# Softmax division, LayerNorm steps, row maximum and load buffers in the attention stage of a streaming encoder layer

## The chip, the cores and the metric

The kernel runs on one core of one Trainium2 chip. A core has a matrix engine (TensorE, PE in the profile; its weight loads are PEld), a vector engine (VectorE, DVE), an activation engine (ScalarE, ACT), a general engine (GpSimd, POOL) and a queue processor (SyncE, SP) which here issues all transfers. The metric is the time of one execution in microseconds (us), lower is better.

## The reference

One layer of a hybrid encoder runs over 1024 prompt frames and 64 sample frames (with 128 cached frames before them), 1088 columns in all. Shown is what matters here:

```
h = x + 1/2 * SwiGLU_1(RMSNorm(x))
u = RMSNorm(h); z = u @ W_in        # q, k, v, indexer q/k/weights, conv input, branch gates
attn:  every query keeps its top-k keys by indexer score, then
       p = softmax(q k^T / 8 over the kept keys); o = p v      # 8 heads of 64, 2 key/value heads
conv:  c = GLU(conv_in); dc = depthwise causal conv(c, width 31)
       conv_out = silu(LayerNorm(dc)) @ conv_w_out             # LayerNorm over 512 channels
merged = sigmoid(g_a) * (attn @ attn_w_out) + sigmoid(g_c) * conv_out
h = h + merged @ W_out
h = h + 1/2 * SwiGLU_2(RMSNorm(h))
y = RMSNorm(h)
```

All is float32. The kernel gets float32 accuracy out of the matrix engine by splitting each operand into a high part and a low remainder (ScalarE copies the high part, VectorE or GpSimd subtracts it) and adding three products: high x high, high x low, low x high (lines 136, 137, 138).

## The kernel before

Channels lie on the 128 partitions, frames along the free axis. Frames are worked in three chunks of 364, 362 and 362 columns (CHUNKS). Weights come tile by tile from DRAM (`raw`), and are split into `whi` (ScalarE, line 118) and `wlo` (GpSimd, line 119).

The program has these stages: the first feed-forward block, the input projection with convolution and indexer, the search for the top-k threshold, then the attention stage, and the second feed-forward block. The change lies in the attention stage alone.

**Attention.** There are nine query tiles (ATILES, in the order TORD = 7, 6, 8, 5, 4, 3, 2, 1, 0; tile i < 8 has 128 queries and 128(i + 1) keys, tile 8 has 64 queries and 192 keys) and four pairs of heads in each: 36 units, class Pair. A unit goes through three functions:

- `soft` (line 1189): for each of the two heads, and for one or two blocks of keys (two blocks when there are more than 512 keys), PE writes logits into a PSUM tile `lg` (lines 1209, 1210; there are three such tiles), and one VectorE instruction (line 1212) adds the mask `bias`, writes `pr` and gives the row maximum of the block into `mb`. Then the maximum is scaled into `mx` (lines 1218, 1220), ScalarE takes the exponential with a row sum `sm` (line 1222), VectorE inverts `sm` (line 1224), and the two heads are divided: the first by GpSimd (line 1225), the second by ScalarE (line 1226).
- `turn` (line 1229): PE transposes up to two blocks of keys of both heads into `pt` (line 1236; two PSUM tiles), and `pt` is split into `ph` (ScalarE) and `pl` (VectorE), both under lines 152 and 153. One such portion is a slot.
- `values` (line 1248): PE multiplies with the values (lines 1256, 1257) into `pv` (one PSUM tile); ScalarE and VectorE make `oh` (lines 1262, 1263), and SP stores it into `d_at` (line 1264).

`attention` (line 1268) runs `soft` two units ahead of `turn` (AHEAD = 2) and `values` two slots behind it (LAG = 2). After each slot it calls `fill`, which runs background steps from a list of five parts, in order. RATE says how many steps go with a slot in each part: 0.5, 1, 1, 0.5, 1.

**The background parts.** 1: `gate_part`, the last four gate projections (three chunks each, 12 steps, lines 1156 to 1164) and the LayerNorm of chunk 2. 2: `conv_part`, `conv_out` of chunks 2, 1, 0 (eight steps each) with the LayerNorms of chunks 1 and 0. 3: `merge` of chunk 2. 4: `wout` of chunk 2. 5: `merge` of chunk 1. What is left runs after the attention. A generator's `yield` ends a step.

`norm` (line 1292) works on the four channel tiles of one chunk: it loads `lx` (line 1298) and adds pairs of tiles on GpSimd (line 1299); takes column sums on PE (lines 166 and 1302) and the mean `mu`; subtracts it and squares, four tiles (lines 1308, 1309), and adds (line 1310); takes column sums again and an inverse square root (lines 185 to 191); and then for four tiles scales, applies swish by tanh and splits into `ch` and `cl` (lines 1321 to 1330), which `conv_out` multiplies with its weights. `both` joins two generators, one step of the second to each step of the first:

```
def both(a, b):
    for _ in a:
        next(b, None)
        yield
    for _ in b:
        yield
```

`conv_out` loads a gate row into `gc`, multiplies, stores it in `d_mp`. `merge` loads `ga` and `mpt`, adds both branches, and splits the sum into `xh` and `xl`. `wout` loads a row `hr` of h, adds to it, and stores it. `gc`, `ga`, `mpt` and `hr` have two buffers each.

**The order of the work** is not that of the program text. A planner reorders instructions on each engine by a priority (program order, and blocks marked as more urgent, such as the weight loads) and by a simulated time line with estimated durations, in which an instruction can be taken once its inputs and its buffers are free. The order it finds is fixed in the program; on the chip each engine works through its own queue in that order and waits where an input is late. All transfers go through the one queue of SP.

Of the kernel before, what the change touches and what calls it, by code (L numbers as in the profile page):

```python
# [9 lines left out]
F32 = mybir.dt.float32  # L10
# [82 lines left out]
class Kern:  # L93
# [432 lines left out]
    def run(self):  # L526
        tc, nc, a = self.tc, self.nc, self.a
        PS = bass.MemoryType.PSUM
        with ExitStack() as top:
# [659 lines left out]
            def soft(u):  # L1189

                rows, L = u.rows, u.L
                if u.h0 == 0 and u.i not in qts:
                    qts[u.i] = load_q(ak, d_q, u.t0, rows)
                qt = qts[u.i]
                nb = 2 if L > 512 else 1
                pw = L // nb
                mb = ap_.tile([P, 2, 2], F32, name="mb", tag="mb", bufs=AHEAD + 1)
                mx = ap_.tile([P, 2], F32, name="mx", tag="mx", bufs=AHEAD + 1)
                sm = ap_.tile([P, 2], F32, name="sm", tag="sm", bufs=AHEAD + 1)
                u.pr = []  # L1200
                kh, kl = K[u.g]
                for hh in range(2):
                    p = ap_.tile([P, 1024], F32, name="pr", tag="pr", bufs=2 * AHEAD + 2)[:rows, :L]
                    u.pr.append(p)
                    q = qt[:, u.h0 + hh, :rows]
                    for b in range(nb):
                        o = lgp.tile([P, 512], F32, name="lg", tag="lg")[:rows, :pw]
                        ks = u.k0 + b * pw
                        nc.tensor.matmul(o, q, kh[:, ks:ks + pw], start=True, stop=False)
                        nc.tensor.matmul(o, q, kl[:, ks:ks + pw], start=False, stop=True)  # L1210
                        bo = BOFF[u.i] + b * pw
                        nc.vector.tensor_tensor_reduce(p[:, b * pw:(b + 1) * pw], o, bias[:rows, bo:bo + pw],
                                                       1.0, -3e38, op0=ALU.add, op1=ALU.max,
                                                       accum_out=mb[:rows, hh, b:b + 1])
                        if (hh, b) == (1, nb - 1):
                            mm = mb[:rows, :, 0]
                            if nb == 2:
                                nc.vector.tensor_tensor(mx[:rows, :], mm, mb[:rows, :, 1], op=ALU.max)
                                mm = mx[:rows, :]
                            nc.vector.tensor_scalar(mx[:rows, :], mm, -0.125, None, op0=ALU.mult)  # L1220
                            for e in range(2):
                                nc.scalar.activation(u.pr[e], u.pr[e], AF.Exp, bias=mx[:rows, e:e + 1],
                                                     scale=0.125, accum_out=sm[:rows, e:e + 1])
                            nc.vector.reciprocal(sm[:rows, :], sm[:rows, :])
                            nc.gpsimd.tensor_scalar(u.pr[0], u.pr[0], sm[:rows, 0:1], None, op0=ALU.mult)
                            nc.scalar.activation(u.pr[1], u.pr[1], AF.Copy, scale=sm[:rows, 1:2])
                        yield

# [63 lines left out]
            def norm(c, lp_, cp_):  # L1292

                c0, w = CHUNKS[c]
                wd = w if c < 2 else w + 30
                x = lp_.tile([P, 4, 392], F32, name="lx", tag="lx")[:, :, :wd]
                s = lp_.tile([P, 4, 392], F32, name="ls", tag="ls")[:, :, :wd]
                nc.sync.dma_start(x, d_dc[:, :, c0:c0 + wd].rearrange("t p w -> p t w"))
                nc.gpsimd.tensor_tensor(s[:, 0:2, :], x[:, 0:2, :], x[:, 2:4, :], op=ALU.add)
                yield  # L1300
                mu = lp_.tile([P, 4], F32, name="mu", tag="mu", bufs=2)
                v = self.colsum([s[:, t, :] for t in range(2)], wd)[:, :, 0]
                mu = mu[:, :v.shape[1]]
                nc.vector.tensor_scalar(mu, v, -1.0 / 512, None, op0=ALU.mult)
                yield
                m = self.spread(mu, wd)
                for t in range(4):
                    nc.vector.tensor_tensor(x[:, t, :], x[:, t, :], m, op=ALU.add)
                    nc.scalar.activation(s[:, t, :], x[:, t, :], AF.Square)
                nc.gpsimd.tensor_tensor(s[:, 0:2, :], s[:, 0:2, :], s[:, 2:4, :], op=ALU.add)  # L1310
                yield
                yield
                y = self.rsqrt(self.colsum([s[:, t, :] for t in range(2)], wd), 1.0 / 512, lp_)
                yield
                yield
                r = self.spread(y, wd)
                ch = cp_.tile([P, 4, WMAX], F32R, name="ch", tag="ch")
                cl = cp_.tile([P, 4, WMAX], F32R, name="cl", tag="cl")
                C[c] = ch, cl
                for t in range(4):  # L1320
                    nc.vector.scalar_tensor_tensor(x[:, t, :], x[:, t, :], par("lng", t), r,
                                                   op0=ALU.mult, op1=ALU.mult)
                    nc.scalar.activation(s[:, t, :], x[:, t, :], AF.Tanh, bias=hb[:, 16 + t:17 + t], scale=0.5)
                    nc.scalar.activation(x[:, t, :], x[:, t, :], AF.Identity, bias=par("lnb", t))
                    nc.vector.scalar_tensor_tensor(x[:, t, :], s[:, t, :], 1.0, x[:, t, :],
                                                   op0=ALU.add, op1=ALU.mult)
                    parts = [(0, w, 0)] if c < 2 else [(0, SEQ - c0, 0), (SEQ - c0, w, 30)]
                    for a0, a1, sh in parts:
                        self.split(ch[:, t, a0:a1], cl[:, t, a0:a1], x[:, t, a0 + sh:a1 + sh],
                                   nc.vector if t % 2 else nc.gpsimd)  # L1330
                yield

            def conv_out(c, lp_):
                c0, w = CHUNKS[c]
                ch, cl = C[c]
                for m in range(8):
                    if m % 2 == 0:
                        wt = self.wload(wc[m // 2], 1024)
                    p = self.psum()[:, :w]
                    self.proj(p, wt, lambda k: ch[:, k, :w], lambda k: cl[:, k, :w], 4, (m % 2) * 512)  # L1340
                    gc = lp_.tile([P, WMAX], F32, name="gc", tag="gc", bufs=2)[:, :w]
                    nc.sync.dma_start(gc, d_g[8 + m, :, c0:c0 + w])
                    nc.vector.scalar_tensor_tensor(gc, gc, 1.0, p, op0=ALU.add, op1=ALU.mult)
                    nc.sync.dma_start(d_mp[m, :, c0:c0 + w], gc)
                    yield
# [7 lines left out]
            def merge(c, mp_):  # L1353
# [9 lines left out]
                for m in range(8):  # L1363
                    if m % 2 == 0:
                        wt = self.wload(wa[m // 2], 1024)
                    ga = mp_.tile([P, WMAX], F32, name="ga", tag="ga", bufs=2)[:, :w]
                    nc.sync.dma_start(ga, d_g[m, :, c0:c0 + w])
                    mpt = mp_.tile([P, WMAX], F32, name="mpt", tag="mpt", bufs=2)[:, :w]
                    nc.sync.dma_start(mpt, d_mp[m, :, c0:c0 + w])
                    p = self.psum()[:, :w]  # L1370
                    self.proj(p, wt, lambda k: ah[:, k, :], lambda k: al[:, k, :], 4, (m % 2) * 512)
                    nc.vector.scalar_tensor_tensor(p, ga, 1.0, p, op0=ALU.add, op1=ALU.mult)
                    nc.vector.scalar_tensor_tensor(ga, mpt, 0.5, p, op0=ALU.mult, op1=ALU.add)
                    self.split(mh[:, m, :w], ml[:, m, :w], ga)
                    yield
# [12 lines left out]

            def h_dram(pool):
                def row(m, c0, w):  # L1390
                    x = pool.tile([P, WMAX], F32, name="hr", tag="hr", bufs=2)[:, :w]
                    nc.sync.dma_start(x, d_h[:, m, c0:c0 + w])
                    return x, lambda: nc.sync.dma_start(d_h[:, m, c0:c0 + w], x)
                return row
# [6 lines left out]
            def both(a, b):  # L1401
                for _ in a:
                    next(b, None)
                    yield
                for _ in b:
                    yield
# [2 lines left out]

            def gate_part():  # L1410
                steps = gates(gorder[GPRE:], ak, 2)
                for _ in range(3 * (16 - GPRE) - 7):
                    next(steps)
                    yield
                lp = C["pool"] = self.pool(cx, "ln", 1)
                yield from both(norm(2, lp, lp), steps)
                act_es.close()

            def conv_part():
# [236 lines left out]
```

## Time and profile before

| | |
|---|---|
| median of 3 runs | 2339.89 us (2335.2 to 2342.22) |
| the profiled execution | 2337.39 us, of which its span is 2335.6 us |
| busy in the span | PE 2250.3, DVE 1689.2, ACT 1390.8, POOL 1499.4 us |
| mean granted clock of TensorE | 0.988 |
| attention stage | about 1180 to 1510 us of the span |

The span goes from the first to the last instruction of the program. A row of a stretch gives its bounds and length, then busy time and count for PE, PEld, DVE, ACT and POOL, the granted clock, the share of the transfer engines and GB/s. A row of a time line gives start, duration, engine, line, operation, output and inputs; in brackets stands the idle time of the engine just before, and what ended it. A row of a group gives the busy time and the mean duration in ns behind the first bar, and the idle time before these instructions with what ended it behind the second. A row for one line gives minimum, median and maximum in ns. A row of waits says who waited for whom, with total us, number of times and the longest.

### The profile page before, as it was taken

The numbers are of one execution on the slowest core, as the hardware profiler recorded it, in microseconds if no ns is written. First come the engines' busy times: TensorE is split into PE (matmuls) and PEld (weight loads), VectorE is DVE, ScalarE is ACT, GpSimd is POOL, SyncE is SP. The second block draws the span as 40 slices with busy tenths as digits, with TensorE's granted clock in tenths as the row PEclk, the third lists the DMA queues.
The fourth block names the chain that finished last, engine by engine and source line by source line (L and its number), as shares of the span: only waits on it lengthen the run. The fifth ranks groups of instructions, "written<-read, shape, count | busy, mean of one in ns | idle before, by whom it ended". The sixth has DMA issues, their size and how long they took to land. (4 is left out here: it accounts for less than half of the span.)

```text
span 2335.6 us, 44194 instructions
## 1 busy us (share of the span) xinstructions
PE 2250.3 (96%) x16226; PEld 2213.6 (95%) x16226; DVE 1689.2 (72%) x3868; ACT 1390.8 (60%) x2883; POOL 1499.4 (64%) x1039
## 2 busy tenths in 40 slices
PE   7999999999999999999999999899999999999997
PEld 6999999999999999999988889899999999999997
DVE  7887766787776388689956777467877757887765
ACT  6655555666546454897446767447656556556553
POOL 5677755677757593788723555467667756667664
PEclk9999999999999999999999999999999999999998
DMA  5322233223223443334322455753223232323233
GB/s 189 109 100 100 100 100 108 99 95 109 100 93 132 143 133 120 93 110 138 120 67 74 144 171 176 238 199 114 91 91 109 95 115 72 112 103 105 100 100 111
DMA packets 129548, 273.40 MB, mean 117 GB/s; under 512 B 17840, under 2 KB 77104, under 8 KB 129328
## 3 DMA queue, kind: packets, MB, share of 16 engines
q1 hardware_dynamic: 129328, 270.56, 35.1%
q8 instruction: 127, 2.08, 0.4%
q14 instruction: 93, 0.76, 0.1%
HBM read 231.82 MB, written 38.75 MB: 116 GB/s over the span
## 5 line engine op out<-in xcount | busy, mean ns | idle before, releaser
L136 PE MATMUL ps<-x,wp 128*128 128x272 f32 x1760 | 508.5, 290 | 7.1 <-ACT spare L342 3.3
L138 PE MATMUL ps<-x,wp 128*128 128x272 f32 x1760 | 504.1, 291 | 3.0 <-DVE wp L153 1.9
L137 PE MATMUL ps<-x,wp 128*128 128x272 f32 x1760 | 506.4, 288 | 0.0
L136 PE MATMUL ps<-x,whi 128*128 128x272 f32 (+2 forms) x1544 | 481.9, 312 | 6.0 <-ACT x L152 2.2
L153 POOL TENSOR_TENSOR wp<-s,wp 128x512 fp32r<-128x512 f32 x272 | 364.9, 1354 | 190.1 <-ACT wp L152 188.2
L138 PE MATMUL ps<-x,wlo 128*128 128x272 f32 (+2 forms) x1544 | 480.7, 312 | 0.0
L137 PE MATMUL ps<-x,whi 128*128 128x272 f32 (+2 forms) x1334 | 411.7, 309 | 1.0 <-POOL x L153 1.0
L327 POOL TENSOR_TENSOR wlo<-raw,whi 128x1024 fp32r<-128x1024 f32 x120 | 290.0, 2417 | 186.2 <-ACT whi L326 172.7
L119 POOL TENSOR_TENSOR wlo<-raw,whi 128x1024 fp32r<-128x1024 f32 (+1 forms) x123 | 279.1, 2272 | 176.8 <-ACT whi L118 166.3
L136 PEld LDWEIGHTS ps<-x,wp 128*128 128x128 f32 x1760 | 331.4, 189 | 11.9 <-ACT spare L342 5.7
L138 PEld LDWEIGHTS ps<-x,wp 128*128 128x128 f32 x1760 | 328.5, 188 | 6.1 <-DVE wp L153 4.0
L137 PEld LDWEIGHTS ps<-x,wp 128*128 128x128 f32 x1760 | 331.9, 189 | 0.0
L136 PEld LDWEIGHTS ps<-x,whi 128*128 128x128 f32 x1544 | 292.2, 189 | 9.1 <-ACT x L152 2.6
L138 PEld LDWEIGHTS ps<-x,wlo 128*128 128x128 f32 x1544 | 292.3, 189 | 1.2
L137 PEld LDWEIGHTS ps<-x,whi 128*128 128x128 f32 x1334 | 253.1, 190 | 2.4 <-POOL x L153 1.3
L152 ACT ACTIVATE wp<-s 128x512 fp32r<-128x512 f32 x272 | 168.0, 626 | 136.3 <-DVE s L314 75.5
L784 POOL TENSOR_TENSOR ac<-ac,pd 128x559 f32<-128x559 f32 (+1 forms) x132 | 192.5, 1459 | 22.8 <-ACT pd L783 15.4
L152 ACT ACTIVATE wp<-ps 128x512 fp32r<-128x512 f32 x208 | 123.2, 592 | 113.6 <-DVE ps L312 100.5
L439 DVE SCALAR_TENSOR_TENSOR h<-ps,h 128x272 f32<-128x272 f32 x448 | 174.1, 429 | 12.9 <-PE ps L138 12.4
L137 PE MATMUL ps<-gl,whi 128*128 128x272 f32 x640 | 183.4, 292 | 0.0
L137 PE MATMUL ps<-gl,wp 128*128 128x272 f32 x640 | 180.9, 288 | 0.0
L136 PE MATMUL ps<-gh,wp 128*128 128x272 f32 x640 | 178.8, 290 | 1.9 <-DVE h L439 1.8
(289 smaller groups left out, 5831.4 us busy)
## 6 DMA issues: line engine op xcount, KB each, us to landing
raw<-wf SPq DMA_DIRECT2D x353, 512.0 KB, 3.3
d_g<-sg SPq DMA_DIRECT2D x32, 181.0 KB, 1.9
d_h<-h SPq DMA_DIRECT2D x2, 2176.0 KB, 10.0
y<-t SPq DMA_DIRECT2D x32, 136.0 KB, 1.8
raw<-wf SPq DMA_DIRECT2D x16, 256.0 KB, 2.6
raw<-d_q SPq DMA_DIRECT2D x32, 128.0 KB, 3.7
raw<-d_qi SPq DMA_DIRECT2D x24, 128.0 KB, 3.0
d_g<-sg SPq DMA_DIRECT2D x16, 182.0 KB, 2.7
```

The lines of the kernel that those rows point to most:

```text
L119: self.weng.tensor_tensor(lo[:, :n], raw[:, :n], hi[:, :n], op=ALU.subtract)
L136: t.matmul(out, wh, xh, start=first, stop=False, skip_group_check=onto)
L137: t.matmul(out, wh, xl, start=False, stop=False, skip_group_check=onto)
L138: t.matmul(out, wl, xh, start=False, stop=last, skip_group_check=onto)
L152: nc.scalar.activation(hi, x, AF.Copy)
L153: (eng or nc.vector).tensor_tensor(lo, x, hi, op=ALU.subtract)
L327: self.weng.tensor_tensor(lo, raw, hi, op=ALU.subtract)
L439: nc.vector.scalar_tensor_tensor(x, p, 0.5, x, op0=ALU.mult, op1=ALU.add)
L784: nc.gpsimd.tensor_tensor(ac, ac, pd, op=ALU.add)
```

## The change

Four edits, all in the attention stage:

- In `soft`, the second block of a head takes the first block's maximum (in `mb`) as the starting value of its own maximum, so the last block's `mb` is the maximum of the row. The two VectorE instructions of lines 1218 and 1220 go; one ScalarE instruction scales `mb` into `mx`. The first head is divided by ScalarE instead of GpSimd.
- In `norm`, a step ends after two of the four tiles of the subtraction and after each of the first three tiles of the last part: it has 11 yields instead of 7.
- `both` takes two steps of the second generator for each step of the first (it now serves `conv_out` with `norm`). In `gate_part`, one gate step goes alone instead of five, and then each step of `norm` comes with one gate step; that makes 12 steps as before.
- `gc`, `ga`, `mpt` and `hr` have three buffers each.

```diff
@@ soft
                         nc.vector.tensor_tensor_reduce(p[:, b * pw:(b + 1) * pw], o, bias[:rows, bo:bo + pw],
-                                                       1.0, -3e38, op0=ALU.add, op1=ALU.max,
+                                                       1.0, mb[:rows, hh, 0:1] if b else -3e38,
+                                                       op0=ALU.add, op1=ALU.max,
                                                        accum_out=mb[:rows, hh, b:b + 1])
                         if (hh, b) == (1, nb - 1):
-                            mm = mb[:rows, :, 0]
-                            if nb == 2:
-                                nc.vector.tensor_tensor(mx[:rows, :], mm, mb[:rows, :, 1], op=ALU.max)
-                                mm = mx[:rows, :]
-                            nc.vector.tensor_scalar(mx[:rows, :], mm, -0.125, None, op0=ALU.mult)
+                            nc.scalar.activation(mx[:rows, :], mb[:rows, :, nb - 1], AF.Copy, scale=-0.125)
                             for e in range(2):
                                 nc.scalar.activation(u.pr[e], u.pr[e], AF.Exp, bias=mx[:rows, e:e + 1],
                                                      scale=0.125, accum_out=sm[:rows, e:e + 1])
                             nc.vector.reciprocal(sm[:rows, :], sm[:rows, :])
-                            nc.gpsimd.tensor_scalar(u.pr[0], u.pr[0], sm[:rows, 0:1], None, op0=ALU.mult)
+                            nc.scalar.activation(u.pr[0], u.pr[0], AF.Copy, scale=sm[:rows, 0:1])
                             nc.scalar.activation(u.pr[1], u.pr[1], AF.Copy, scale=sm[:rows, 1:2])
@@ norm
                     nc.scalar.activation(s[:, t, :], x[:, t, :], AF.Square)
+                    if t == 1:
+                        yield
                 nc.gpsimd.tensor_tensor(s[:, 0:2, :], s[:, 0:2, :], s[:, 2:4, :], op=ALU.add)
...
                         self.split(ch[:, t, a0:a1], cl[:, t, a0:a1], x[:, t, a0 + sh:a1 + sh],
                                    nc.vector if t % 2 else nc.gpsimd)
+                    if t < 3:
+                        yield
                 yield
@@ conv_out; the same in merge for ga and mpt, in h_dram for hr
-                    gc = lp_.tile([P, WMAX], F32, name="gc", tag="gc", bufs=2)[:, :w]
+                    gc = lp_.tile([P, WMAX], F32, name="gc", tag="gc", bufs=3)[:, :w]
@@ both
                 for _ in a:
                     next(b, None)
+                    next(b, None)
                     yield
@@ gate_part
-                for _ in range(3 * (16 - GPRE) - 7):
+                for _ in range(3 * (16 - GPRE) - 11):
                     next(steps)
                     yield
                 lp = C["pool"] = self.pool(cx, "ln", 1)
-                yield from both(norm(2, lp, lp), steps)
+                ns = norm(2, lp, lp)
+                for _ in ns:
+                    next(steps, None)
+                    yield
                 act_es.close()
```

More of the change, by code (lines that the diff above doesn't have):

```diff
@@ L1365, in merge @@
                         wt = self.wload(wa[m // 2], 1024)
-                    ga = mp_.tile([P, WMAX], F32, name="ga", tag="ga", bufs=2)[:, :w]
+                    ga = mp_.tile([P, WMAX], F32, name="ga", tag="ga", bufs=3)[:, :w]
                     nc.sync.dma_start(ga, d_g[m, :, c0:c0 + w])
-                    mpt = mp_.tile([P, WMAX], F32, name="mpt", tag="mpt", bufs=2)[:, :w]
+                    mpt = mp_.tile([P, WMAX], F32, name="mpt", tag="mpt", bufs=3)[:, :w]
                     nc.sync.dma_start(mpt, d_mp[m, :, c0:c0 + w])
@@ L1390, in row @@
                 def row(m, c0, w):
-                    x = pool.tile([P, WMAX], F32, name="hr", tag="hr", bufs=2)[:, :w]
+                    x = pool.tile([P, WMAX], F32, name="hr", tag="hr", bufs=3)[:, :w]
                     nc.sync.dma_start(x, d_h[:, m, c0:c0 + w])
```

## The prediction

> **What bounds the kernel now.** I read the page first, then stretches by stage.
>
> ```profile
> span 2335.6 us, 44194 instructions
> PE 2250.3 (96%) x16226; PEld 2213.6 (95%) x16226; DVE 1689.2 (72%) x3868; ACT 1390.8 (60%) x2883; POOL 1499.4 (64%) x1039
> ```
> ```profile
> core 0: us, PE busy (x) PEld busy (x) DVE busy (x) ACT busy (x) POOL busy (x), PEclk, DMA share, GB/s
> 1180.00:1260.00 80.00, 76.14 (x485) 73.75 (x484) 43.66 (x124) 46.68 (x77) 28.07 (x12) 0.96 0.18 58
> 1260.00:1400.00 140.00, 125.29 (x806) 115.84 (x804) 103.85 (x292) 97.15 (x202) 71.93 (x40) 0.95 0.49 146
> 1400.00:1510.00 110.00, 97.20 (x606) 93.46 (x607) 69.60 (x183) 69.31 (x154) 57.19 (x34) 0.96 0.64 197
> 1600.00:2336.00 736.00, 716.35 (x5633) 710.69 (x5631) 541.12 (x1184) 422.10 (x919) 478.94 (x331) 0.99 0.30 101
> ```
> PE sets the pace: outside the attention stage it is idle a few per cent at a clock of 0.99. The change touches 1180 to 1510, where PE is idle 3.9 + 14.7 + 12.8 = 31.4 us and the clock is down to 0.95. No edit removes PE work, so the gain can only come from idle PE and lost clock. Next, the single waits of PE, in order of time, and three stretches at half clock:
>
> ```profile
> start us, us, engine line op out<-in xcount [idle before <-releaser]
> 1276.38 0.59 PE L136 MATMUL ps<-ch,whi 128*128 128x362 f32 x2 [2.42 <-ACT ch L152]
> 1280.90 0.48 PE L1236 MATMUL pt<-ident,pr 128*128 128x128 f32 x1 [3.02 <-DVE pl L153]
> ...
> 1319.18 0.45 PE L1209 MATMUL lg<-kh,qt 128*128 128x384 f32 x1 [1.15 <-DVE mb L1212]
> 1323.65 0.69 PE L1236 MATMUL pt<-ident,pr 128*128 128x128 f32 x2 [2.07 <-POOL pr L1225]
> ...
> 1338.35 0.82 PE L166 MATMUL ps<-ones,ls 128*128 128x128 f32 x5 [1.02 <-POOL ls L1299]
> ...
> 1370.73 0.77 PE L136 MATMUL ps<-ch,whi 128*128 128x364 f32 x2 [1.82 <-ACT ch L152]
> ...
> 1422.49 0.44 PE L1209 MATMUL lg<-kh,qt 128*128 128x384 f32 x1 [1.45 <-DVE mb L1212]
> 1433.28 0.38 PE L1209 MATMUL lg<-kh,qt 128*128 128x256 f32 x1 [1.87 <-DVE mb L1212]
> ```
> ```profile
> 1278.80:1285.70 6.90, 4.80 (x19) 4.73 (x19) 4.57 (x9) 3.34 (x9) 3.63 (x6) 0.51 0.61 188
> 1323.20:1326.60 3.40, 2.95 (x12) 2.95 (x13) 0.83 (x4) 3.38 (x10) 3.40 (x3) 0.50 0.02 5
> 1371.00:1374.40 3.40, 2.92 (x13) 2.48 (x13) 3.34 (x7) 3.40 (x8) 3.23 (x3) 0.50 0.24 61
> ```
> The waits of 1276, 1319 to 1323 and 1370 are the ends of the three LayerNorms, where all four tiles are normalised in one background step; each is followed by half clock. At half clock half of PE's busy time is lost: (4.80 + 2.95 + 2.92) / 2 = 5.3 us.
>
> **The change part by part.** *LayerNorm in single tiles.* The same instructions are issued; between tiles now lies other work. At 1276 conv_out waits 2.42 for the last `ch`; with one tile per step only that tile's chain is left, I take 1.8 back. At 1280 the transposes wait 3.02 behind `cl` on DVE:
>
> ```profile
> L153 DVE TENSOR_TENSOR cl<-lx,ch x8: 316/720/2524, 1277.0 to 1375.2; 128x298 fp32r<-128x298 f32 x2, 128x64 fp32r<-128x64 f32 x2, 128x362 fp32r<-128x362 f32 x2, 128x364 fp32r<-128x364 f32 x2
> ```
> The slowest took 2.52 against a median of 0.72; with the four no longer in one heap I take 2.1 back. At 1319 I take half of 1.15 (0.6). At 1338 and 1370 the next norm runs two steps per conv_out step and is done two steps ahead of its reader: 1.0 and 1.8. Together 7.3 us. What is moved in the queues: each of the two later norms sends its one load to SP earlier among the loads and stores of conv_out, and its POOL additions and subtractions earlier among the weight subtractions, about 2 us each; conv_out's own transfers wait that much longer, covered by its two to three buffers, at no cost as long as the weights are loaded some steps ahead. If that cover were gone, the next weight would be late by one POOL subtraction, some 2 us. The first norm starts four gate steps sooner; its load and first addition stand at 1150 already (rival 3), so that alone changes nothing.
>
> *Both divides on ScalarE.*
>
> ```profile
> L1225 POOL TENSOR_SCALAR pr<-pr,sm 128x1024 f32<-128x1024 f32 (+8 forms) x36 | 60.8, 1691 | 99.7 <-DVE sm L1224 80.5 <-PE pt L1236 6.7 <-DVE ps L191 2.5
> L1226 ACT ACTIVATE pr<-pr,sm 128x1024 f32<-128x1024 f32 (+8 forms) x36 | 26.4, 735 | 6.1 <-DVE sm L1224 6.0
> L552 ACT ACTIVATE hb<-par x2: 189/194/198, 15.6 to 15.7; 128x16 f32<-128x16 f32 x1, 128x4 f32<-128x4 f32 x1
> 1360.00:1380.00 20.00, 17.33 (x104) 15.25 (x103) 17.78 (x43) 18.62 (x39) 11.15 (x7) 0.91 0.41 122
> ```
> POOL loses 60.8 us, off the path but for the 2.07 at 1323, where ACT would itself need about one more divide: I take 2.07 - 0.74 = 1.3, rounded down to 1.1. ACT gains 36 divides of 0.735 (26.4) and 36 `mx` scalings at the 0.19 of the small `hb` rows (7.0): 33.4 us in 330, or 2.0 in every 20. ACT's free time covers it (43 us in 1260 to 1400, 41 in 1400 to 1510), but 18.62 of 20 at 1360 leaves nothing over. Queued behind a divide on ACT stand the evictions of transposes (`ph`), on which PE's next values wait. Bounds: 0 to half exposed (17); I take 2, nearer the cover.
>
> *Running row maximum.*
>
> ```profile
> L1220 DVE TENSOR_SCALAR mx<-mb 128x2 f32<-128x2 f32 (+1 forms) x20 | 9.8, 492 | 0.1
> L1218 DVE TENSOR_TENSOR mx<-mb 128x2 f32<-128x2 f32 x16 | 5.8, 364 | 0.2
> L1220 DVE TENSOR_SCALAR mx<-mx 128x2 f32<-128x2 f32 x16 | 4.0, 248 | 0.2
> 1430.29 2.16 DVE L1220 TENSOR_SCALAR mx<-mb 128x2 f32<-128x2 f32 x1
> 1430.06 2.37 POOL L119 TENSOR_TENSOR wlo<-raw,whi 128x1024 fp32r<-128x1024 f32 x1
> 1353.85 0.16 DVE L190 SCALAR_TENSOR_TENSOR rt<-rt,ps 128x3 f32<-128x3 f32 x1
> 1354.04 0.17 DVE L191 SCALAR_TENSOR_TENSOR ps<-rt,ps 128x3 f32<-128x3 f32 x1
> 1357.85 0.07 DVE L1212 DVE_READ_ACCUMULATOR2_ANT mb<- 128x1 f32 x1
> 1357.85 0.48 DVE L1212 CUSTOM_DVE_ANT_0 pr<-lg,bias 128x320 f32<-128x320 f32 x1
> ```
> DVE loses 9.8 + 5.8 + 4.0 = 19.6 us. Two numbers a row cost up to 2.16, and that one ended with the 2.37 of POOL's weight subtraction: it held `mb`, and so the 1.87 of PE at 1433. In exchange the second reduction of a head (32 of them: four tiles, four pairs, two heads) must wait for the accumulator of the first. Independent ones start with the read of 0.08; dependent small ones (1353.85, 1354.04) stand 0.03 apart after the end: 32 x 0.11 = 3.5 us. The net 16 us of DVE lies beside PE: nothing but the wait at 1433.
>
> The Trainium skill (SBUF — State Buffer, Who interferes with whom) says that a GpSimd instruction and a DVE instruction that reads SBUF through both ports shut each other out for a whole instruction, while ACT never waits; the 2.16 agrees. By that rule alone the divide's going would also free all of DVE from POOL; the weight subtractions (2.37) stay, so the sum does not take it.
>
> *Three buffers.* At 1422 DVE sat behind a load of `ga`, and `lg` behind DVE:
>
> ```profile
> DVE ps L1372 <- DMA ga<-d_g: 4.9, 6, 1.7
> DVE hr L1385 <- DMA hr<-d_h: 13.5, 3, 4.9
> SPq L1369 <- DVE ga L1373: 6.8, 7, 2.0
> SPq L1367 <- DVE oh L1263: 7.2, 3, 3.2
> 1440.00:1480.00 40.00, 39.82 (x255) 39.42 (x253) 14.43 (x37) 19.59 (x35) 25.57 (x14) 1.00 0.61 188
> ```
> A third buffer frees the 6.8 that SP waits for a slot, not the 7.2 behind an attention store. `hr` waits 13.5, but in 1440 to 1480 PE is never short (39.82 of 40): nothing. Of 1.45 + 1.87 = 3.3 at 1422 and 1433 I take 2.5.
>
> *Sum.* 7.3 + 1.1 (divide) + 2.5 = 10.9; of the 5.3 of clock 4.1, since a wait of 1 to 2 us will be left somewhere; less 2 for ACT: 13.0 us. The profiled execution took 2337.4 (1.8 around its span): 2324.4. It lies 2.5 under the median 2339.9, so **2327**. Bounds: all six waits of 1276 to 1370 (11.5), the clock (5.3) and the 3.3 make 20.1 and give 2319.8; none of them, with 17 for ACT, gives 2357.
>
> The Trainium skill (TensorE: Matmul & The Clock Gate, Rules for kernel authors) lets the clock fall only after about 3 us of idle PE. Here the half clock of 1371 follows a wait of 1.82 and that of 1323 one of 2.07, so the measurement decides. By the rule two of the three dips would not belong to these waits, and an estimate would keep 2.9 us less.
>
> **The rivals.**
> 1. *The waits only move* (0.20). The planner fits other work into each gap by estimated durations, and `ps` has two banks; after the spreading, DVE's or ACT's queue makes PE wait elsewhere. For: 1422 and 1433 are such waits without any LayerNorm. Against: 1440 to 1480 has none. Only the buffers' 2.5 remain: 2337.
> 2. *ACT becomes what the transposes wait for* (0.12), the slower side. Place: the eviction `ph`, queued behind two divides of one pair. It decides from the point where ACT's free time in a slice is less than the 2.0 added, as at 1360 to 1380 with 1.4. Were the whole stretch from 1260 to 1400 like that, its share of the new work, 33.4 x 140 / 330 = 14.2 us, would lie on the path, two more half clocks of 3.4 us would cost 3.4, and LayerNorm would gain nothing: 2337.4 + 14.2 + 3.4 - 2.5 for the buffers = 2352.5, on the median 2355. For: that slice, where PE is down to 17.33. Against: ACT is idle 43 of 140, and the softmax runs two pairs ahead of its transposes, so a late divide has time in hand.
> 3. *A norm's first sum stands too close behind its load* (0.08). Two norm steps now go with one conv_out step, so load, add and column sum come together.
>
> ```profile
> DMA to landing us min/median/max: 4.6/4.8/5.7
> L1299 POOL TENSOR_TENSOR ls<-lx x3: 1738/1757/1868, 1150.6 to 1336.6; 128x784 f32<-128x784 f32 x1, 128x724 f32<-128x724 f32 x1, 128x728 f32<-128x728 f32 x1
> ```
> PE would wait up to 4.8 + 1.8 = 6.6 twice, with half clock 16.6, against the 13 of the sum: 2341, on the median 2343. For: 1.02 at 1338 with a step between. Against: the planner moved the first norm's add to 1150, ahead of the whole stage.
> 4. *All of it comes* (0.10): the 20.1 of the bound, and with a lighter DVE half of what else PE waits in 1400 to 1510 (12.8 - 3.3 = 9.5): 2339.9 - 24.9 = 2315. For: DVE is busy 104 of 140 in the LayerNorm stretch, and loses a part of that. Against: the waits behind attention's own stores and sums stay as they are.
> 5. *The third buffers do nothing*, since SP is one queue: 2.5 us less, 2329, inside the forecast's own range.
>
> **How the numbers follow.** The forecast has 0.50, its own range 2319 to 2334. Within 0.3% (7 us, about what this kernel's runs can tell) of 2340 ends at 2333. Faster: 0.10 of case 4, 0.46 of the forecast: 0.56. Same: its other 0.04, the 0.20, 0.03 of case 3: 0.27. Slower: 0.12 and 0.05: 0.17. For 8 in 10 the range goes from 2312 (case 4, with 3 for the spread of the runs) to 2346 (case 3 with the same 3; case 2 is left out).
>
> **What would show it.** Right: no wait on `ch` at the start of a conv_out, a clock of at least 0.97 in the LayerNorm stretch, no `mx` row on DVE, ACT near 247 us in the stage (213 + 33.4), PE idle there near 22 (31.4 - 10.9 + 2). Wrong: PE waiting for ACT `ph` or `pr`, for `ls` before a column sum, or as many half-clock stretches as before.

## The result and the profile after

| | before | after |
|---|---|---|
| median of 6 runs | 2339.96 us (2335.2 to 2344.19) | 2320.26 us (2312.97 to 2326.88) |
| ratio | | 0.9919, 95% interval 0.9898 to 0.9940 |
| the profiled execution, its span | 2337.39, 2335.6 us | 2322.28, 2320.5 us |

The kernel became 19.7 us faster (2339.96 - 2320.26), by the interval between 14 and 24. The forecast was 2327 with a range of 2312 to 2346: the time lies in the range, and the gain is half as large again as the forecast's 13. The two profiled executions differ by only 15.1 us; the one of after took 2.0 us more than its median.

The page of the kernel after, its span and engines:

```profile
span 2320.5 us, 44122 instructions
PE 2244.1 (97%) x16226; PEld 2213.2 (95%) x16226; DVE 1672.9 (72%) x3816; ACT 1415.6 (61%) x2955; POOL 1440.0 (62%) x1003
```

The attention stage as one stretch, from the first logits to 1.0 us after the start of the last sum `oh`, in the columns of the prediction's stretches; first the kernel before, then the kernel after:

```profile
1178.00:1508.60 330.60, 299.12 (x1898) 283.28 (x1899) 217.13 (x599) 213.19 (x434) 159.20 (x86) 0.96 0.46 141
```
```profile
1175.20:1494.00 318.80, 295.63 (x1898) 283.46 (x1899) 204.63 (x547) 237.47 (x506) 99.36 (x50) 0.95 0.48 148
```

The same 1898 matmuls take 318.8 us instead of 330.6: 11.8 of the 15.1. Of this, idle PE is 8.3 (31.5 against 23.2); the other 3.5 lie in PE's busy time, whose ends the profile models. 2.8 us came before the stage, where the order of PE is the same in both kernels, so they belong to the execution and not to the change. DVE lost 12.5, POOL 60, ACT gained 24.3. (The 36 divides and 36 scalings last 33 us by their rows, but an ACT instruction starts some 0.09 us before the one ahead of it ends, so the busy time grows by less.)

What PE waited for in the stage after the change (who, for whom, total us, times, longest):

```profile
PE lg L1209 <- DVE mb L1212: 7.5, 5, 4.4
PE ps L136 <- ACT ah L152: 5.0, 3, 2.3
PE pv L1253 <- DVE oh L1260: 4.9, 3, 2.7
PE lg L1209 <- ACT sg L1162: 1.8, 1, 1.8
PE ps L166 <- POOL ls L1296: 1.7, 1, 1.7
PE ps L136 <- DVE oh L1260: 1.6, 1, 1.6
PE pt L1233 <- DVE pl L153: 1.6, 2, 0.9
```

There is no wait for `ch` any more (4.2 us in two waits before), none for the divided `pr` (2.1), and the one for `pl` is down to 1.6 (3.2). The wait for `ls` before a column sum has grown from 1.0 to 1.7, now with half clock behind it, and the one for `ah` from 2.7 to 5.0. Half clock itself is not less: six stretches begin at 1185, 1314, 1386, 1461, 1468 and 1488, together 34 us, where six began at 1187, 1279, 1323, 1371, 1402 and 1504 before, together 31 us. A time line of PE and the six stretches of the kernel after:

```profile
1313.82 1.42 PE L166 MATMUL ps<-ones,ls 128*128 128x128 f32 x7 [1.72 <-POOL ls L1296]
...
1488.72 0.58 PE L1253 MATMUL pv<-ph,vt 128*128 128x256 f32 x1 [2.66 <-DVE oh L1260]
1491.02 0.58 PE L1253 MATMUL pv<-ph,vt 128*128 128x256 f32 x1 [1.50 <-DVE oh L1260]
1493.43 0.67 PE L136 MATMUL ps<-xh,whi 128*128 128x362 f32 x1 [1.62 <-DVE oh L1260]
```
```profile
1184.80:1191.60 6.80, 6.16 (x18) 5.60 (x19) 4.25 (x13) 3.86 (x6) 0.00 (x0) 0.51 0.00 0
1314.30:1317.70 3.40, 3.40 (x17) 3.40 (x16) 0.36 (x2) 0.86 (x2) 0.00 (x0) 0.50 0.20 60
1386.00:1392.80 6.80, 5.61 (x21) 5.22 (x22) 5.45 (x14) 6.72 (x16) 3.02 (x2) 0.50 0.06 16
1461.10:1464.50 3.40, 3.40 (x13) 2.86 (x14) 1.62 (x9) 3.37 (x13) 0.00 (x0) 0.50 0.12 35
1467.90:1471.30 3.40, 3.40 (x14) 3.15 (x14) 1.62 (x5) 3.09 (x13) 0.39 (x1) 0.50 0.07 19
1488.40:1498.60 10.20, 6.75 (x21) 6.17 (x22) 3.27 (x5) 1.75 (x4) 1.84 (x1) 0.50 0.93 306
```

How far the background work moved ahead is seen in the multiplication that ends each `conv_out` step (minimum, median and maximum in ns, then first and last start); before, then after:

```profile
L1343 DVE SCALAR_TENSOR_TENSOR gc<-gc,ps x24: 514/532/535, 1286.8 to 1396.4; 128x362 f32<-128x362 f32 x16, 128x364 f32<-128x364 f32 x8
```
```profile
L1344 DVE SCALAR_TENSOR_TENSOR gc<-gc,ps x24: 500/532/534, 1273.4 to 1372.4; 128x362 f32<-128x362 f32 x16, 128x364 f32<-128x364 f32 x8
```

`conv_out` ends 24.0 us earlier, the last store of attention only 11 to 15 (1508.6 to 1497.3 for its issue, 1507.6 to 1493.0 for the sum it stores). At the end of the stage, from 1485.7 to 1493.4, PE has attention's `pv` alone, and waits for `oh` to empty the one `pv` tile.

### The profile page after: what moved, and what is told of

It is laid out like the page before. It is cut to its first block, busy times and chain, and to the rows that moved or that the text cites. A ratio compares the mean times of both kernels' runs of the same rounds, so it can differ in the third digit from the quotient of the medians.

```text
span 2320.5 us, 44122 instructions
## 1 busy us (share of the span) xinstructions
PE 2244.1 (97%) x16226; PEld 2213.2 (95%) x16226; DVE 1672.9 (72%) x3816; ACT 1415.6 (61%) x2955; POOL 1440.0 (62%) x1003
```

## The experiments

All times are ratios to the kernel before on the same chip, with 95% intervals; 0.001 is 2.3 us. The first four take one edit alone, the next four leave one edit out of the whole change, the last four test what came out of these.

| kernel | divide | maximum | LayerNorm | buffers | ratio | interval |
|---|---|---|---|---|---|---|
| s_ln | | | x | | 0.9965 | 0.9952 to 0.9978 |
| s_div | x | | | | 1.0042 | 1.0030 to 1.0055 |
| s_max | | x | | | 0.9991 | 0.9982 to 1.0000 |
| s_buf | | | | x | 0.9983 | 0.9972 to 0.9994 |
| l_div | | x | x | x | 0.9945 | 0.9931 to 0.9958 |
| l_ln | x | x | | x | 0.9975 | 0.9966 to 0.9984 |
| l_max | x | | x | x | 0.9977 | 0.9967 to 0.9987 |
| l_buf | x | x | x | | 0.9960 | 0.9947 to 0.9973 |
| p_dm | x | x | | | 1.0038 | 1.0025 to 1.0051 |
| the change | x | x | x | x | 0.9919 | 0.9898 to 0.9940 |

### LayerNorm steps alone (s_ln)

```diff
 def both(a, b):
     for _ in a:
         next(b, None)
+        next(b, None)
         yield
```
together with the yields in `norm` and the loop of `gate_part`; all else as before.

> LayerNorm steps alone (single tiles, two norm steps per conv_out step). The prediction's own terms: 7.3 us of waits and 4.1 of clock come back, 11 us, ratio 0.995, and no wait of PE on ch. Rival, the waits only move: within 4 us of before, with as much idle PE in the stage (31 us). Second rival, the gain needs the freed DVE and POOL: ln alone under 5 us.

Measured: 0.9965, 8 us faster (5 to 11), near the 11 of the terms. PE's waits for `ch` are gone in its trace, as forecast. Idle PE in the stage is hardly less (29.7 us, from 324.60 and 294.93 in the row below, against 31.5): PE now waits 6.3 us for `ga` (2.3 before) and 5.7 for `ah` (2.7). But the clock is higher: 0.97 in the stage, with 17 us at half clock against 31, and over all runs a mean of 0.9900 against 0.9868 of the kernel before on the same chip. This difference alone, 0.0032 of 2345 us, is 7.5 us.

```profile
1178.40:1503.00 324.60, 294.93 (x1899) 281.56 (x1900) 220.70 (x597) 212.50 (x434) 155.87 (x86) 0.97 0.47 142
```

So the waits did move, as the rival had it, yet into pieces that cost less clock. For idle PE this rests on one execution, which took 5 us less than the median of its kernel.

### Both divides on ScalarE alone (s_div)

```diff
-nc.gpsimd.tensor_scalar(u.pr[0], u.pr[0], sm[:rows, 0:1], None, op0=ALU.mult)
+nc.scalar.activation(u.pr[0], u.pr[0], AF.Copy, scale=sm[:rows, 0:1])
```

> Both divides on ScalarE alone, all else as before. The prediction's terms: 2 us of exposed ACT against 1.1 us for the wait on POOL at 1323: 1 us slower, ratio 1.000. Rival, ACT becomes what the transposes wait for: 8 to 14 us slower, PE waiting for ACT pr or ph. Rival, the POOL divide held VectorE by the shared port and held the transposes more than the waits show: 5 us faster or more.

Measured: 1.0042, 10 us slower (7 to 13): inside the first rival's 8 to 14. PE's waits in its trace:

```profile
PE pt L1236 <- DVE pl L153: 14.8, 9, 3.3
PE pv L1256 <- DVE oh L1263: 6.1, 4, 3.6
```

and the longest of the nine, with what ACT did before it:

```profile
1373.13 0.69 PE L1236 MATMUL pt<-ident,pr 128*128 128x128 f32 x2 [3.29 <-DVE pl L153]
```
```profile
1369.36 0.59 ACT L1323 ACTIVATE ls<-lx,hb 128x364 f32<-128x364 f32 x1
1369.85 0.82 ACT L1225 ACTIVATE pr<-pr,sm 128x640 f32<-128x640 f32 x1
1370.57 0.81 ACT L1226 ACTIVATE pr<-pr,sm 128x640 f32<-128x640 f32 x1
1371.28 0.59 ACT L1324 ACTIVATE lx<-lx,par 128x364 f32<-128x364 f32 x1
1371.77 0.58 ACT L152 ACTIVATE ph<-pt 128x512 fp32r<-128x512 f32 x1
```

ACT runs without a break, both divides of a pair between two LayerNorm instructions, and the eviction `ph`, without which VectorE cannot form `pl`, comes late. This is the prediction's second rival, true for the edit alone, although its sign, PE waiting for `ph` or `pr`, did not come: PE's waits are put down to `pl`. Not all nine have this cause. Before the wait of 3.07 that ended at 1327.23, `ph` was done at 1324.19; VectorE came to `pl` only at 1326.41, since two instructions ahead of it ran beside GpSimd subtractions and took 1.93 and 0.90 us (their medians in the kernel before are 0.53 and 0.16).

The expectation's last rival falls: GpSimd has 61 us less to do in the stage (159.2 to 97.7), and VectorE's busy time is 219.2 us against 217.1, so by this sum the divide on GpSimd had not held VectorE up.

### Running maximum alone (s_max)

```diff
-1.0, -3e38, op0=ALU.add, op1=ALU.max,
+1.0, mb[:rows, hh, 0:1] if b else -3e38, op0=ALU.add, op1=ALU.max,
...
-nc.vector.tensor_scalar(mx[:rows, :], mm, -0.125, None, op0=ALU.mult)
+nc.scalar.activation(mx[:rows, :], mb[:rows, :, nb - 1], AF.Copy, scale=-0.125)
```

> Running row maximum with the scaling on ScalarE alone. The prediction's terms: 16 us less VectorE, worth only the 1.9 us wait of 1433: 2 us faster, ratio 0.999. Rival, the two small VectorE rows set how late mb frees lg and exp starts: 6 us faster or more. Rival, waiting for the accumulator costs more than 0.11 us each: slower.

Measured: 0.9991, 2 us faster (0 to 4), as the terms had it, though the interval reaches to no gain.

### Three buffers alone (s_buf)

```diff
-gc = lp_.tile([P, WMAX], F32, name="gc", tag="gc", bufs=2)[:, :w]
+gc = lp_.tile([P, WMAX], F32, name="gc", tag="gc", bufs=3)[:, :w]
```
and the same for `ga`, `mpt` and `hr`.

> Three buffers alone. The prediction's terms: about 1 us (the wait of 1422), ratio 0.9995. Rival, the single SP queue makes them useless: 0. Rival, loads that start earlier free VectorE in the merge steps: 5 us faster.

Measured: 0.9983, 4 us faster (1 to 7). DVE's waits for these loads, 22.6 us before (13.5 for `hr`, 4.9 for `ga`, 4.2 for `gc`), shrink to one of 0.8 for `ga` and one of 0.8 on a store of `gc`. So one queue on SP does not make the third buffers useless: the loads do land earlier. But DVE then waits longer for PE (17.2 us against 9.3 before the sum into `hr`), so 21 us bought 4, and 4 us is no more than another order of the same work may give (c_swap, below).

### Leaving one edit out (l_div, l_ln, l_max, l_buf)

Each is the kernel after with the one edit undone.

> The whole change but for the divide, which stays on GpSimd for the first head. If the edits' effects simply multiply (divide alone 1.0042, whole change 0.9919), this is 0.988, the fastest so far. Theory that the divide on ScalarE pays once the LayerNorm heaps and the small VectorE rows are gone: slower than the whole change, 0.994 to 0.998. Rival, the divide is then worth nothing either way: 0.992.

> The whole change but for the LayerNorm steps. If the effects multiply: 0.995. Theory that the divide costs what it does because it queues with the LayerNorm heaps on ScalarE: 1.000 or slower, with PE waiting for the evictions pl and ph of transposes 10 us or more, as with the divide alone (14.8). Rival, the running maximum is what makes room on the softmax path: 0.994 or faster.

> The whole change but for the running maximum; the maximum and its scaling stay on VectorE. If the effects multiply: 0.993. Theory that the round trip ScalarE, VectorE, ScalarE for mx matters once ScalarE has both divides: 0.997 or slower, with ScalarE waiting for mx 20 us or more (24.9 with the divide alone). Rival, it is worth nothing: 0.992.

> The whole change but for the third buffers. If the effects multiply: 0.9936. Theory of the prediction, a small term: 0.9925. Rival, with the background ahead of the attention the loads matter more: 0.996 or slower.

Multiplied, the four single ratios give 0.9981 (4 us); the whole change gives 0.9919. So the edits do not add up, they need one another. Added last, the LayerNorm steps take the time from 0.9975 to 0.9919, the running maximum from 0.9977, the buffers from 0.9960, and the divide from 0.9945. The first three intervals lie clear of the whole change's; that of the divide does not. The loss of 10 us that the divide brings alone is gone in this company, but a gain by it is not shown.

Of the expectations, that of l_div (0.994 to 0.998) has its number. Without the LayerNorm steps (l_ln) the time is slower than multiplying gives, but neither 1.000 nor a wait of 10 us for `pl` came: 0.9975, and 6.5 us. Without the buffers (l_buf) the rival came, at 0.9960: beside the other edits the loads matter more than the prediction's small term.

What the maximum does beside both divides is seen where it is left out (l_max): ACT waits for `mx`, and the scalings on VectorE take up to 2.3 us. First the waits of ACT, then the rows of the scaling:

```profile
ACT pr L1222 <- DVE mx L1220: 17.8, 12, 2.7
```
```profile
L1220 DVE TENSOR_SCALAR mx<-mb x20: 148/156/1817, 1273.8 to 1476.5; 128x2 f32<-128x2 f32 x16, 64x2 f32<-64x2 f32 x4
L1220 DVE TENSOR_SCALAR mx<-mx x16: 159/169/2321, 1189.2 to 1361.2; 128x2 f32<-128x2 f32 x16
```

The expectation wanted 0.997 or slower, which 0.9977 meets, and 20 us of ACT's waits, of which 17.8 is short. After the change, ACT still waits 15.6 us, for `mb` itself, so the waiting is hardly less; the row that scales is now even:

```profile
ACT mx L1217 <- DVE mb L1212: 15.6, 7, 5.9
```
```profile
L1217 ACT ACTIVATE mx<-mb x36: 186/192/206, 1187.5 to 1472.8; 128x2 f32<-128x2 f32 x32, 64x2 f32<-64x2 f32 x4
```

### Divide and maximum together (p_dm)

The kernel before with the diffs of s_div and s_max.

> Before with two edits: both divides on ScalarE and the running maximum with its scaling on ScalarE. If the effects multiply: 1.0033. Theory that the two are a pair (the whole softmax between the maximum and the row sum stays on ScalarE, and the divide's loss alone came from ScalarE waiting for mx, 24.9 us): 0.997 to 1.000, with PE waiting for pl under 7 us, against 14.8 with the divide alone. Rival, the LayerNorm heaps on ScalarE are what makes the divide cost: 1.003, with PE waiting for pl about 15 us.

Measured: 1.0038, where multiplying gives 1.0033. The theory that these two are a pair falls. Its trace has the wait of the divide alone:

```profile
PE pt L1233 <- DVE pl L153: 15.5, 8, 3.5
```

Its three longest, 3.5, 3.2 and 2.8 us, all have both divides of a pair among the last four instructions of ACT ahead of the late `ph`; LayerNorm's stand there in one. The longest, with its rows of VectorE and of ACT:

```profile
1395.86 0.44 PE L1233 MATMUL pt<-ident,pr 128*128 128x128 f32 x2 [3.50 <-DVE pl L153]
```
```profile
1391.68 0.54 DVE L1340 SCALAR_TENSOR_TENSOR gc<-gc,ps 128x364 f32<-128x364 f32 x1 [2.27 <-DMA gc<-d_g]
1392.13 0.16 DVE L1221 RECIPROCAL sm<-sm 128x2 f32<-128x2 f32 x1
```
```profile
1392.32 0.72 ACT L1222 ACTIVATE pr<-pr,sm 128x512 f32<-128x512 f32 x1 [2.38 <-DVE sm L1221]
1392.95 0.71 ACT L1223 ACTIVATE pr<-pr,sm 128x512 f32<-128x512 f32 x1
1393.56 1.04 ACT L118 ACTIVATE whi<-raw 128x1024 fp32r<-128x1024 f32 x1
1394.51 1.06 ACT L152 ACTIVATE ph<-pt 128x512 fp32r<-128x512 f32 x2
```

Adding the LayerNorm steps to it (l_buf, 0.9960) or the buffers (l_ln, 0.9975) takes the loss away; the wait for `pl` goes to 1.1 and 6.5 us. For the LayerNorm steps this agrees with the rival of the expectation, that the heaps on ACT make the divide cost, and its number came; but the rows above show the divides late without such a heap. Why the buffers, worth 0.0017 alone, are worth 0.006 here is not settled. They bring no work off ACT, and the whole plan of the stage is another one. One path is seen above: VectorE stands 2.27 us for a load of `gc`, the inverse `sm` and with it both divides come late, and `ph` after them. VectorE waits 13.5 us for loads of `gc` and `ga` in p_dm, and 2.1 with the third buffers (l_ln).

### The scaling on VectorE (m_dve)

```diff
-nc.scalar.activation(mx[:rows, :], mb[:rows, :, nb - 1], AF.Copy, scale=-0.125)
+nc.vector.tensor_scalar(mx[:rows, :], mb[:rows, :, nb - 1], -0.125, None, op0=ALU.mult)
```
in the kernel after.

> The whole change, but mx is scaled on VectorE from the running maximum (one small VectorE instruction more for each pair of heads, one ScalarE instruction less). If the round trip by VectorE and its lock against GpSimd's weight subtractions are what the running maximum removes: 0.995 or slower, with single mx rows of 1 us and more. If the one small VectorE instruction that goes with two blocks, or the bare reordering, is what counts: 0.992, as the whole change.

Measured: 0.9954 (0.9940 to 0.9969). The rows of more than 1 us are back:

```profile
L1217 DVE TENSOR_SCALAR mx<-mb x36: 148/163/2142, 1194.5 to 1472.4; 128x2 f32<-128x2 f32 x32, 64x2 f32<-64x2 f32 x4
```

The ratio and the rows meet the first expectation (0.995 or slower), and the interval only touches that of the whole change, so most of the 0.006 of the maximum may lie in this one small instruction. It is not shown: in the profiled executions the attention stage is not made longer by it (316.5 us here, 318.8 in the whole change), and the next kernel moves the time by 0.002 with nothing of weight changed.

### The divides in the other order (c_swap)

```diff
-nc.scalar.activation(u.pr[0], u.pr[0], AF.Copy, scale=sm[:rows, 0:1])
-nc.scalar.activation(u.pr[1], u.pr[1], AF.Copy, scale=sm[:rows, 1:2])
+nc.scalar.activation(u.pr[1], u.pr[1], AF.Copy, scale=sm[:rows, 1:2])
+nc.scalar.activation(u.pr[0], u.pr[0], AF.Copy, scale=sm[:rows, 0:1])
```

> The whole change with the two ScalarE divides in the other order (second head first). Nothing that any theory names is different; the planner makes another order from it. If the differences between the kernels come from named mechanisms: 0.990 to 0.994. If the planner's lottery alone moves the time as much as the edits: outside 0.988 to 0.996.

Measured: 0.9941 (0.9928 to 0.9954), a hair outside what named mechanisms allow and well inside the other bound, so the expectation does not decide. Nothing of weight is different, yet compared row by row some 550 of the 16226 matmuls stand elsewhere in PE's order. The interval overlaps that of the whole change, and one reordering is one sample; as a rough measure, a difference of 0.002 to 0.003 between two kernels of this family can be the planner's order or the spread of the runs alone. By this measure the LayerNorm steps (0.9975) and the maximum (0.9977) stand out within the whole; the buffers (0.9960) less; the divide (0.9945) and the place of the scaling (0.9954) are not told from a reordering, nor are the maximum and the buffers each alone (0.9991, 0.9983).

### Background work kept for the tail (x_tail)

```diff
 def wout_part():
-    yield from wout(2, h_dram(self.mp))
+    C["wo"] = wout(2, h_dram(self.mp))
+    for _ in range(6):
+        next(C["wo"])
+        yield
 def last_part():
     yield from merge(1, self.mp)
+    yield from C["wo"]
...
-for c0, w in CHUNKS[::-1]:
+for c0, w in (CHUNKS[1], CHUNKS[2], CHUNKS[0]):
     nc.sync.dma_start(h[:, :, c0:c0 + w], d_h[:, :, c0:c0 + w])
```

> The whole change, with the last two wout steps of chunk 2 kept back until merge of chunk 1 is issued, and h loaded for chunk 1 first. The trace after has PE waiting 10 us between 1450 and 1495, where the background work has run out, and half clock for 17 us there. If lack of background work is what the tail lacks: 5 to 8 us faster than the whole change, 0.989. Rival, the tail waits for oh and d_at whatever stands behind: 0.992. Rival, h comes back later by the held-back stores and the second feed-forward block starts late: 0.994 or slower.

Measured: 0.9928 (0.9916 to 0.9941), not told apart from the whole change. In its trace most of the waiting for `oh` at the tail is gathered into one place; its row, and what ACT did before it:

```profile
1491.83 0.67 PE L136 MATMUL ps<-xh,whi 128*128 128x362 f32 x1 [3.69 <-DVE oh L1260]
```
```profile
1490.55 0.51 ACT L152 ACTIVATE ah<-ar 128x364 fp32r<-128x364 f32 x1 [1.67 <-DMA ar<-d_at]
1490.96 0.36 ACT L1259 ACTIVATE oh<-pv 64x256 f32<-64x256 f32 x1
```

The `pv` waits of 1488 to 1491 (4.2 us) are filled but for 1.9 us, and PE then waits 3.7 for the last `oh`. Its inputs are not late: the last `xl` was done at 1483.5. By the program this matmul is the first in the eight PSUM tiles that the kernel opens once attention's eight are closed, so the last `pv` must have been read. Its matmuls ended at 1488.1, but `oh` stands on ACT behind `ah`, which waits for attention's own output to come back from `d_at`. Between 1440 and 1500 PE waits 9.9 us, against 10.4 in the whole change: the wait only moved, as the second rival had it.

## Why the prediction was right, and where it was wrong

**The number** came near in part by luck. The sum adds four terms as if each stood alone; measured alone, the four edits multiply to a gain of 4 us, not 13. What makes 20 of them is how they act on one another, and no term holds that. The way, and the place where the time comes back, were forecast for a reason.

**PE as the bound** was right: every engine but ACT lost work, PE's matmuls stayed, and idle PE in the stage fell from 31.5 to 23.2, near the 22 that was named. ACT came to 237.5 us in the stage and not to 247, because its instructions overlap by some 0.09 us each.

**Two of the signs of being wrong came all the same**: PE waits 1.7 for `ls` before a column sum, and the stage has as many stretches of half clock as before, six. The step that failed there is "of the 5.3 of clock 4.1": in the one profiled execution none of it came back over the stage (0.95 against 0.96), and four of the six stretches are at new places. Over the six runs of the whole change the mean clock is 0.9893, against 0.9868 to 0.9881 in the three sets of runs of the kernel before; on 2340 us this is an estimated 3 to 6 us, so some of the clock did come. The mark of 0.97 in the LayerNorm stretch was not reached (0.96 from 1257 to 1397).

**LayerNorm in single tiles** (7.3 us of waits, 4.1 of clock): right in sum, 8 us alone and 13 within the whole (0.9975 to 0.9919). Its signs came as named: no wait on `ch`, none on `pr`. The split into waits and clock was wrong for the edit alone, where the clock gave nearly all. One reading was wrong as well: the `cl` of 2.52 us at 1277 was not slow from standing in a heap, it ran beside a weight subtraction of GpSimd (1276.82 to 1279.17). The slowest `cl` after the change still takes 2.47, beside another one, and yet PE's longest wait for `pl` is 0.9 where it was 3.02: what was won there is the order of the work, not a faster `cl`.

**The divide** ("I take 2, nearer the cover", less 1.1 for the wait of 1323): mis-sized. Alone it costs 10 us, since ACT's free time as a whole (43 of 140) is no cover where both divides of a pair stand in the queue right ahead of `ph`, with LayerNorm's heaps or a weight copy beside them. The bound of 17 held this. Within the whole the small figure fits, since nothing of the divide is told from a reordering there: the LayerNorm steps or the buffers, either of them, take most of the loss away. The terms were written as if they were independent.

**The running maximum** (the 1.87 at 1433): right alone, 2 us, mis-sized within the whole, where it is worth 13 (0.9977 to 0.9919). The trace of the whole change has no DVE row for `mx`, as named. The dependent reductions cost less than was taken: 0.747 against 0.687 for 512 columns, 0.06 each, where 0.11 stood with the wait. Its mechanism within the whole is not settled: ACT waits for the maximum nearly as long as before, and m_dve is not told from a reordering. How the 7 us by which the forecast was short divide among the edits is not shown either, since the four values do not add up.

**The buffers** (at most the 1.45 at 1422): mis-sized, 4 us alone, about 10 within the whole (0.9960 to 0.9919). The sentence that `hr`, covered by a full PE, is worth nothing looked at the wait's own place; a DVE that is not stopped at a load does what stands behind it earlier, as the path through `sm` in p_dm shows for `gc`.

**The rivals.** The first (the waits only move) holds in part for LayerNorm alone. The second was true of s_div and p_dm and false of the whole. The third came in its place and small: 1.72 before the column sum at 1313, against the 6.6 it could have cost. The fourth (all of it comes, 2315) is near in its number, 2320, and not in its way: idle PE fell by 8.3 us, not by the 11.5 + 3.3 of the waits named, and behind 1400 only from 12.8 (to 1510) to 10.4 (to 1494). The fifth falls by VectorE's waits for its loads. That background work would run out at the tail, and give part of the gain back, is in no rival: PE's waits after 1485 are 5.8 us, with 10.2 us at half clock.

## What to carry to other kernels

Edits that relieve different engines of one stage are not a sum: here one of them costs 10 us alone and nothing that can be seen beside the other three, and another is worth 2 alone and 13 beside them. Before an instruction is moved to an engine with idle time, look at what it will stand ahead of in that engine's queue in the worst 20 us, and break such heaps first. With a planner that reorders everything, time a neutral reordering too: the one tried here moved this kernel by 0.002, hardly more than the spread of its runs, and differences of that size explain nothing.

## What had not been expected of the hardware

The clock falls after short waits and stays down for 3.4, 6.8 or 10.2 us: behind a wait of 1.72 us the kernel after ran at 0.50 from 1314.3 to 1317.7, with PE busy throughout. (The rule of about 3 us that the prediction set aside stands in the Trainium skill, TensorE: Matmul & The Clock Gate, under Why this matters for your kernels; this wait goes against it too.) Not every such wait does it. After 1.76 us at 1175 in the kernel after, and 1.87 at 1433 in the kernel before, the clock stayed at 1.00, while the stretch of 1467.9 has only waits of 0.39 and 0.76 just ahead of it. Half of the time at half clock is 15 us before, 17 after and 8.5 in s_ln, beside 31.5, 23.2 and 29.7 us of idle PE: an estimated 0.3 to 0.7 us of lost clock with each microsecond of waiting. And a VectorE instruction on two numbers a row, 0.16 us by its median before, took up to 2.1 to 2.3 us in every kernel that has it, the longest always beside one of GpSimd's weight subtractions of 2.4 us.
